# First norm of a diffusion trunk: sums of squares on VectorE, x/rms ahead of the modulation, products by feature tile, fixed orders

## The chip, the cores and the metric

The kernel runs on one core of a Trainium2 chip, in one launch. The metric is device microseconds of one execution; lower is better. Before the change three runs took 1626.13, 1631.45 and 1633.98 us, so the median is 1631.45 us.

## The reference, cut to what matters

The model is a trunk of two layers over 512 latent tokens (x) and 256 context tokens (ctx), with 1024 features, all in float32. Every sub-layer begins with an RMSNorm that is modulated by the conditioning vector:

```python
def rmsnorm(x, g):
    y = xf * lax.rsqrt(jnp.mean(xf * xf, axis=-1, keepdims=True) + NORM_EPS)
    return y * g
def modulate(h, shift, scale):
    return h * (1 + scale) + shift
...
mod_x = jnp.split(jax.nn.silu(c) @ ada_w[layer] + ada_b[layer], 6)
mod_c = jnp.split(jax.nn.silu(c_ctx) @ ada_w[layer] + ada_b[layer], 6)
h_x = modulate(rmsnorm(x, norm_g[layer, 0]), mod_x[0], mod_x[1])
h_c = modulate(rmsnorm(ctx, norm_g[layer, 0]), mod_c[0], mod_c[1])
# layer 0: projections of h_x and h_c by w_in, then differential and neighbourhood attention
```

The change touches only the start of layer 0: the modulation's shift and scale for the first norm, the norm of x and of ctx, and the first unit of projected queries, keys and values (a unit is two pairs of heads, 128 columns each of key and query, 256 of value for the first pair of units).

## The kernel before, in words

Everything lies with features on the 128 partitions, so x is 8 tiles (k = 0 to 7) of 128 features by 512 tokens and ctx is 8 tiles of 128 by 256. A product in full precision is made of three fp32r matmuls: the operand and the weight are each split into a high part and the rest, and high·high, high·rest and rest·high are added in PSUM (`wh`, `wl` are the two parts of a weight tile, `hb[k][:, 0]` and `hb[k][:, 1]` those of a feature tile).

The start of layer 0 runs like this. SyncE's queue loads x, then the modulation's weights in two halves of eight 512 KB tiles (`add_ada0(0)` and `add_ada0(1)`; each half gives shift and scale of four feature tiles, for x and ctx), with the three weight tiles of the first unit (key, query, value) between the halves and the context between those. ScalarE squares the x tiles (`sq_sum`, L324) and VectorE and GpSimd add them up; TensorE sums over partitions with a matrix of ones, and `rstd_of` (L308) makes 1/rms of it with Ln, Exp and a Newton step. `ada0_mm` (L640) multiplies the modulation tiles as they land, `ada0_h` (L647) copies the result out, transposes it, adds the bias (L249), forms the scale (L257), and calls `h_make` (L348) for each of four feature tiles: VectorE makes x times scale times 1/rms (L353), ScalarE adds the shift and rounds to the high part (L354), VectorE makes the rest (L355). `part` (L663) then multiplies those four tiles with the unit's key and query weights (512 columns wide, L667 to L669) and its value weights (256 columns, L675 to L677). Then come the sum of squares and norm of ctx, its first four tiles, the modulation's second half, the other four tiles of x, `part` again, and the last four of ctx. `keep_busy` (L212) issues products of the identity with ones whose result nobody reads.

Behind this stand, for the first unit, `qk_x` (L716: rotation by `rope_of`, L376, and splitting by `evac_pair`, L364), `qk_c` (L724: the key's, then the query's products with the context, L207 to L209, and their splitting), `v_group` (L390: the values of the context), and then the steady program of attention steps with the projections of later units between them.

Each engine runs its own queue in order. The framework that builds the program puts the instructions of each engine in an order by its own plan, from the order of the Python code and from what waits for what; `tc.issue_after(inst)` makes an instruction stand behind another in that plan. Before the change the order in this place is left to the plan. Tiles come from pools with a fixed number of buffers; a new tile waits until the readers of the tile that had its buffer are through. The one that matters here is the PSUM pool of the linear products, with two buffers:

```python
lin = st.enter_context(tc.tile_pool(name="a_lin", bufs=2, space=PSUM, reuse_waits="tile"))
linp = lambda: lin.tile([P, NX], F32, tag="lin", name="lin")
...
psk, psq = linp(), linp()
```

So the key's context products need the buffer of `psk`, which the rotation reads (L380, L381), the query's that of `psq`, and `v_group` again the buffer of the key's context products.

## Time and profile before

| what | value |
|---|---|
| median of three runs | 1631.45 us |
| the profiled execution | 1634.54 us |
| its span, first to last instruction | 1632.7 us |
| TensorE busy with matmuls | 1569.6 us, 96% of the span |
| VectorE, ScalarE, GpSimd busy | 1255.6, 747.0, 267.0 us |
| chain that ended last | TensorE 64%, VectorE 7%, DMA 4% |
| mean granted TensorE clock | 0.992 |

A profile page gives busy time per engine and shows the span in 40 equal slices (40.8 us each here), a digit for each slice in tenths of busy time. The timeline lists instructions: start and length in us, engine (PE is TensorE, DVE VectorE, ACT ScalarE, POOL GpSimd), line of the kernel, operation, output and inputs by their names in the program, shapes, and in brackets the idle time of the engine just before it and what ended that. A fp32 matmul is two records, a fp32r matmul one. The windows view gives, for stretches of the span, the busy time of each engine with the number of instructions, the granted clock (PEclk), the share of the DMA engines' time and GB/s.

### The profile page before, as it was taken

How to read it: one execution, taken by the hardware profiler on the slowest of the kernel's cores; microseconds unless marked ns; L12 is line 12 of the kernel's file. 1: busy time of each engine (PE TensorE's matmuls, PEld its weight loads, DVE VectorE, ACT ScalarE, POOL GpSimd, SP SyncE). 2: the span in 40 equal slices, each digit the busy share in tenths (PEclk: the TensorE clock that was granted, in tenths of full speed). 3: DMA queues.
4: the chain of work that ended last, by engine and by line, in shares of the span. 5: the costliest groups of instructions: out<-in, count | busy, mean ns of one | idle time of the engine just before them, and what ended most of it. 6: DMA issues, size and time to landing. Idle time of an engine off the chain costs nothing.

```text
span 1632.7 us, 26333 instructions
## 1 busy us (share of the span) xinstructions
PE 1569.6 (96%) x10222; PEld 1403.5 (86%) x10222; DVE 1255.6 (77%) x2157; ACT 747.0 (46%) x1324; POOL 267.0 (16%) x311
## 2 busy tenths in 40 slices
PE   5899998998999999999999999999999999999997
PEld 3798887886878899999999998887788899989897
DVE  4757698976688888978899867787665887869686
ACT  4446554555334532432424244456655542524344
POOL 2222222345010000010100011264322000000001
PEclk9999999999999999999999999999999999999999
DMA  9322244544235365576766753311010442323321
GB/s 343 98 57 85 89 149 129 186 139 132 72 109 154 95 183 158 152 197 168 195 180 169 211 134 95 104 53 40 14 40 27 152 132 66 125 82 104 117 78 52
DMA packets 69220, 198.48 MB, mean 122 GB/s; under 512 B 6900, under 2 KB 19348, under 8 KB 69096
## 3 DMA queue, kind: packets, MB, share of 16 engines
q1 hardware_dynamic: 59464, 164.40, 31.7%
q0 software_dynamic: 9056, 31.87, 9.1%
q8 instruction: 81, 1.33, 0.3%
q10 hardware_dynamic: 576, 0.52, 0.1%
q14 instruction: 43, 0.35, 0.1%
HBM read 160.45 MB, written 4.86 MB: 101 GB/s over the span
## 4 chain that ended last, share of the span: by engine, by line
PE 64%; DVE 7%; DMA 4%; issue 2%; ACT 2%; POOL 0%; DVEq 0%; SPq 0%; ACTq 0%; POOLq 0%
PE f L1272 5%; PE f L1274 5%; PE f L1273 5%; PE f L1685 4%; PE f L1684 4%; PE f L1683 4%; PE f L1313 3%; PE f L1314 3%; PE f L1315 3%; PE t L1517 2%; PE lin L207 2%; PE lin L208 2%; PE lin L209 2%; PE f L1737 2%; PE f L1736 2%; PE f L1738 2%
## 5 line engine op out<-in xcount | busy, mean ns | idle before, releaser
L196 ACT ACTIVATE wh<-raw 128x1024 fp32r<-128x1024 f32 (+1 forms) x96 | 92.3, 978 | 233.7 <-DVE raw L507 115.8
L207 PE MATMUL lin<-hb,wh 128*128 128x512 f32 (+1 forms) x456 | 162.8, 358 | 8.2 <-DVE q L372 2.2
L208 PE MATMUL lin<-hb,wh 128*128 128x512 f32 (+1 forms) x456 | 160.3, 352 | 0.5 <-DVE hb L197 0.4
L209 PE MATMUL lin<-hb,wl 128*128 128x512 f32 (+1 forms) x456 | 158.9, 348 | 0.0
L197 DVE TENSOR_TENSOR wl<-raw,wh 128x1024 fp32r<-128x1024 f32 (+1 forms) x96 | 106.8, 1119 | 34.9 <-ACT wh L196 32.9
L269 DVE SCALAR_TENSOR_TENSOR junk<-raw,tables 128x1024 bf16<-128x1024 f32 x80 | 97.7, 1222 | 20.2 <-DMA raw<-in_ada_wT_dram 19.9
L202 POOL DMA_DIRECT2D wl<-raw x39 | 34.1, 873 | 444.1 <-ACT wl L201 393.8
L207 PEld LDWEIGHTS lin<-hb,wh 128*128 128x128 f32 x456 | 86.4, 190 | 23.4 <-issue 4.5
L1313 PE MATMUL f<-g,wh 128*128 128x512 f32 (+1 forms) x304 | 102.8, 339 | 1.2 <-DVE q L1298 0.7
L1314 PE MATMUL f<-g,wh 128*128 128x512 f32 (+1 forms) x304 | 102.7, 339 | 0.0
L1684 PE MATMUL f<-hb,wh 128*128 128x256 f32 x360 | 101.7, 283 | 0.0
L1683 PE MATMUL f<-hb,wh 128*128 128x256 f32 x360 | 101.4, 283 | 0.0
L1685 PE MATMUL f<-hb,wl 128*128 128x256 f32 x360 | 101.2, 283 | 0.0
L1315 PE MATMUL f<-g,wl 128*128 128x256 f32 (+1 forms) x304 | 100.8, 336 | 0.0
L158 ACT CAST wh<-raw 128x1024 fp32r<-128x1024 f32 x61 | 63.9, 1047 | 77.9 <-PE lin L208 24.0
L1272 PE MATMUL f<-hb,wh 128*128 128x384 f32 x288 | 96.4, 335 | 0.9 <-ACT q L1259 0.9
L159 DVE TENSOR_TENSOR wl<-raw,wh 128x1024 fp32r<-128x1024 f32 x61 | 79.8, 1309 | 22.6 <-ACT wh L158 22.4
L208 PEld LDWEIGHTS lin<-hb,wh 128*128 128x128 f32 x456 | 86.7, 190 | 12.2 <-issue 0.9
L1274 PE MATMUL f<-hb,wl 128*128 128x384 f32 x288 | 96.3, 334 | 0.0
L1273 PE MATMUL f<-hb,wh 128*128 128x384 f32 x288 | 96.2, 334 | 0.0
L209 PEld LDWEIGHTS lin<-hb,wl 128*128 128x128 f32 x456 | 86.6, 190 | 10.4 <-issue 0.3
L339 POOL TENSOR_TENSOR ns_a<-ns_a,ns_s 128x256 f32<-128x256 f32 (+1 forms) x16 | 16.2, 1013 | 435.2 <-ACT ns_s L335 435.2
(395 smaller groups left out, 4948.7 us busy)
## 6 DMA issues: line engine op xcount, KB each, us to landing
raw<-in_w_dram SPq DMA_DIRECT2D x132, 512.0 KB, 3.7
raw<-in_ada_wT_dram SPq DMA_DIRECT2D x80, 512.0 KB, 4.2
wl<-raw POOLq DMA_DIRECT2D x39, 512.0 KB, 5.9
raw<-in_w_ab_dram SPq DMA_DIRECT2D x24, 512.0 KB, 4.2
raw<-in_ada_w_dram SPq DMA_DIRECT2D x16, 512.0 KB, 9.5
k<-k SPq DMA_DIRECT2D x16, 384.0 KB, 5.8
raw<-in_w_c_dram SPq DMA_DIRECT2D x12, 512.0 KB, 3.6
nb<-in_na_bias_dram POOLq DMA_DIRECT2D x16, 256.0 KB, 3.6
```

Source lines behind the costliest of these rows:

```text
L207: nc.tensor.matmul(ps, wh(k), xh(k), start=k == 0, stop=False)
L208: nc.tensor.matmul(ps, wh(k), xl(k), start=False, stop=False)
L209: end = nc.tensor.matmul(ps, wl(k), xh(k), start=False, stop=k == n - 1)
L1272: nc.tensor.matmul(ps, wh(k), b[:, 0, :], start=k == 0, stop=False)
L1273: nc.tensor.matmul(ps, wh(k), b[:, 1, :], start=False, stop=False)
L1274: nc.tensor.matmul(ps, wl(k), b[:, 0, :], start=False, stop=k == 3)
L1313: nc.tensor.matmul(ps, hi, g[:, 0, cols[v]], start=first, stop=False)
L1314: nc.tensor.matmul(ps, hi, g[:, 1, cols[v]], start=False, stop=False)
L1315: nc.tensor.matmul(ps, lo, g[:, 0, cols[v]], start=False, stop=last)
L1683: nc.tensor.matmul(ps, wh(k), b[:, 0, :], start=k == 0, stop=False)
L1684: nc.tensor.matmul(ps, wh(k), b[:, 1, :], start=False, stop=False)
L1685: nc.tensor.matmul(ps, wl(k), b[:, 0, :], start=False, stop=k == 3)
```

## The change

It does these things, all in the first norm and the first unit:

- The partial sums of squares of x are added by VectorE alone (`shared=False`), and the last square goes to TensorE as a third addend (`apart=True`) instead of being added first. The conditioning row is loaded and its Silu taken ahead of the squares.
- x/rms is made by itself (`scaled`), with one VectorE multiplication for each tile: four tiles ahead of the modulation's copy, four behind the first half's feature tiles. The modulation is then applied by ScalarE (`x_h`), once for the high part and once into a tile of its own, and VectorE subtracts. ctx keeps `h_make`.
- TensorE gets 44 `keep_busy` products at the start, 4 before and 14 behind the first half's transposes; the 9 behind the second half's go.
- The products run by feature tile (`part_kq(k)`, `part_v(k)`), with the second half's modulation tiles multiplied between those of k = 0 to 3.
- The loads follow one chain on SyncE's queue (`S.chain`): both halves of the modulation, then the last value weights, the context and the rotation's tables (before on GpSimd's queue, and ctx ahead of the second half). The modulation's tiles have 6 buffers of their own (before 5, and 3 of the weights' pool).
- The norm of ctx comes behind the second half: its squares stand behind tile 5's feature tile and `part_v(5)`, all eight of its tiles behind the x products; `qk_x` stands behind the last of them (`queued(h_made[-1][1])`). Scratch tiles lie in buffers of the first unit's own tiles (`Places`).

```diff
+    @contextmanager
+    def queued(*insts):
+        with ExitStack() as q:
+            for i in insts:
+                if i is not None:
+                    q.enter_context(tc.issue_after(i.ins))
+            yield
...
-            ps = ada0_mm(0)
-            rx = rstd_of(tp(), sq_sum(xr, p0), D, p0)
-            ada0_h(0, ps)
-            keep_busy(tp(), 10)
...
+            keep_busy(psk, 44)
...
+            def x_h(k, after=None):
+                t = p0.tile([P, NX], F32, tag="ns_h", name="ns_h", bufs=2)
+                with queued(after):
+                    for z in (hx[k][:, 0, :], t):
+                        act = nc.scalar.activation(z, xn[k], AF.Identity, bias=mod[0][:, 0, 0, k : k + 1], scale=amod[0][:, 0, 0, k : k + 1])
+                    return act, nc.vector.tensor_sub(hx[k][:, 1, :], t, f32(hx[k][:, 0, :]))
+
+            def scaled(ks, after=None):
+                for k in ks:
+                    with queued(after):
+                        end = nc.vector.tensor_mul(xn[k], xr[k], rx)
+                return end
...
+            ps = tp()
+            ada0_mm(ps, range(2))
+            rx = rstd_of(tp(), sq_sum(xr, px, apart=True, shared=False), D, px)
+            end, act = roots
+            four = scaled(range(4))
+            end = ada0_mm(ps, range(2, KT), end)
+            keep_busy(psk, 4, end)
+            flip, made = ada0_mod(0, ps, four)
+            keep_busy(psk, 14, flip)
...
+            last = x_h(3)
+            scaled(range(4, KT), last[1])
...
-            part(range(4))
-            rc = rstd_of(tp(), sq_sum(cr, p0), D, p1)
-            for k in range(4):
-                h_make(k, hc[k], cr[k], rc, 0, 0, 1, p0)
-            ada0_h(1, ada0_mm(1))
-            keep_busy(tp(), 9)
-            wv.append(tuple(wslice(t, 256) for t in S.next()))
-            part(range(4, KT))
-            for k in range(4, KT):
-                h_make(k, hc[k], cr[k], rc, 0, 0, 1, p0)
+            ps = tp()
+            part_kq(0)
+            ada0_mm(ps, (0,), part_v(0))
+            part_kq(1)
+            ada0_mm(ps, (1, 2), part_v(1))
+            part_kq(2)
+            ada0_mm(ps, (3, 4), part_v(2))
+            ada0_mm(ps, (5, 6, 7), part_kq(3))
+            part_v(3)
...
+            _, made = ada0_mod(1, ps)
+            ends = [x_h(k) for k in range(4, KT)]
...
+            part_kq(4)
+            part_v(4)
+            part_kq(5)
+            end = part_v(5)
+            with queued(*ends[1], end):
+                rc = rstd_of(tp(), sq_sum(cr, pc_), D, pc_)
+            part_kq(6)
+            part_kq(7)
+            ctx_h(range(KT))
+            part_v(6)
+            part_v(7)
...
-        qk_x(0, "k", psk)
-        qk_x(0, "q", psq)
+        with queued(h_made[-1][1]):
+            qk_x(0, "k", psk)
+            qk_x(0, "q", psq)
```

Behind this stretch the queues of all engines hold the same instructions in the same order as before, but for a few rows.

Three places show what moves. The first is VectorE at the end of the norm of x (`ns_v`, `ns_t`, `ns_y`, after the change `scratch`, are the steps of 1/rms; `res` is x; `ada_acc` is the copy of the modulation's first half). Before:

```order
L317 TENSOR_SCALAR ns_v_246<-t_221 128x512 [waits Activation_49]
L320 SCALAR_TENSOR_TENSOR ns_t_248<-ns_t_248,ns_v_246 128x512 [waits DVE_49,Activation_49]
L321 SCALAR_TENSOR_TENSOR ns_y_247<-ns_t_248,ns_y_247 128x512 [waits DVE_49]
L649 COPY ada_acc_255<-t_172 128x256 [waits PE_49,Pool_49]
L249 TENSOR_TENSOR mod0_116<-t_257,adab_102 128x2x2 [waits DMASW0_49,PE_49]
```

After:

```order
L351 SCALAR_TENSOR_TENSOR scratch_156<-scratch_154,scratch_156 128x512 [waits DVE_49]
L733 TENSOR_TENSOR scratch_158<-res_73,scratch_156 128x512 [waits DMAHW2_49,DVE_49]
L733 TENSOR_TENSOR scratch_158<-res_74,scratch_156 128x512 [waits DMAHW3_49]
L733 TENSOR_TENSOR scratch_158<-res_75,scratch_156 128x512 [waits DMAHW4_49]
L733 TENSOR_TENSOR scratch_159<-res_76,scratch_156 128x512 [waits DMAHW5_49]
L718 COPY ada_acc_306<-t_224 128x256 [waits PE_49]
L267 TENSOR_TENSOR mod0_117<-t_308,adab_104 128x2x2 [waits DMASW0_49,PE_49]
```

Four multiplications now stand between the last step of 1/rms and the copy.

The second is VectorE at the end of the norm of ctx (`ns_h` and `hb4` to `hb7` with 256 columns are ctx's tiles 4 to 7; `ru` and `rbuf` are the rotation's first two steps, `lin` is `psk` and then `psq`). Before:

```order
L353 SCALAR_TENSOR_TENSOR ns_h_591<-res_81,amod0_118,ns_y_410 128x256 [waits DVE_49]
L355 SCALAR_TENSOR_TENSOR hb4_128<-ns_h_587,mod0_116,hb4_128 128x256 [waits Activation_49]
L380 STREAM_SHUFFLE ru_633<-lin_304 128x512 [waits PE_49]
L355 SCALAR_TENSOR_TENSOR hb5_129<-ns_h_591,mod0_116,hb5_129 128x256 [waits Activation_49]
L381 TENSOR_TENSOR rbuf_147<-lin_304,tables_115 128x512 [waits DMASW6_49]
L353 SCALAR_TENSOR_TENSOR ns_h_595<-res_82,amod0_118,ns_y_410 128x256 [waits DMAHW0_49,DVE_49]
L353 SCALAR_TENSOR_TENSOR ns_h_599<-res_82,amod0_118,ns_y_410 128x256 [waits DVE_49]
L355 SCALAR_TENSOR_TENSOR hb6_130<-ns_h_595,mod0_116,hb6_130 128x256 [waits Activation_49]
L355 SCALAR_TENSOR_TENSOR hb7_131<-ns_h_599,mod0_116,hb7_131 128x256 [waits Activation_49]
L380 STREAM_SHUFFLE ru_642<-lin_305 128x512 [waits PE_49,Pool_49]
```

After:

```order
L385 SCALAR_TENSOR_TENSOR hb6_130<-ns_h_604,mod0_117,hb6_130 128x256 [waits Activation_49]
L385 SCALAR_TENSOR_TENSOR hb7_131<-ns_h_608,mod0_117,hb7_131 128x256 [waits Activation_49]
L410 STREAM_SHUFFLE ru_666<-lin_160 128x512 [waits PE_49]
L411 TENSOR_TENSOR rbuf_147<-lin_160,tables_71 128x512 [waits DMAHW3_49]
L410 STREAM_SHUFFLE ru_675<-lin_161 128x512 [waits PE_49,Pool_49]
L411 TENSOR_TENSOR rbuf_147<-lin_161,tables_71 128x512
L402 SCALAR_TENSOR_TENSOR k1_663<-rbuf_147,k1_663 64x512 [waits Activation_49] x2
L167 TENSOR_TENSOR wl_837<-raw_830,wh_836 128x1024 [waits DMAHW5_49,PE_49,Activation_49]
```

The key's rotation stood among ctx's tiles and now stands behind the last of them.

The third is TensorE between the unit's x products and `v_group` (`s` takes the values of x; `lin` with 256 columns takes the products with ctx). Before, the end of the query's context products and what follows:

```order
L209 MATMUL lin_685<-hb7_131,wl_297 128x256
L675 MATMUL s_306<-wh_511,hb4_128 128x256 [waits Activation_49]
L676 MATMUL s_306<-wh_511,hb4_128 128x256
L675 MATMUL s_307<-wh_511,hb4_128 128x256
L676 MATMUL s_307<-wh_511,hb4_128 128x256
L677 MATMUL s_306<-wl_512,hb4_128 128x256 [waits DVE_49]
```

After, the end of the x values and the start of the key's context products:

```order
L776 MATMUL s_162<-wl_506,hb7_131 128x256
L774 MATMUL s_163<-wh_505,hb7_131 128x256
L775 MATMUL s_163<-wh_505,hb7_131 128x256
L776 MATMUL s_163<-wl_506,hb7_131 128x256
L224 MATMUL lin_687<-hb0_124,wh_330 128x256 [waits DVE_49,Activation_49]
```

The 48 value products of tiles 4 to 7 stood behind both sets of context products and now stand ahead of them; the first context product waits for VectorE.

More of the change, by code (lines that the diff above doesn't have):

```diff
@@ L1 @@
-from contextlib import ExitStack
+from contextlib import ExitStack, contextmanager
 import concourse.bass as bass
@@ L76, in tile_trunk @@
     nc.sync.dma_start(craw, cT)
+    tables = const.tile([P, 2 * NX], F32, name="tables")
+    cost, sint = tables[:, 0:NX], tables[:, NX : 2 * NX]
+    nc.sync.dma_start(tables[0:2, :], crow)
     res_tile = lambda: xpool.tile([P, NX], F32, tag="res", name="res", bufs=KT + KT // 2 + 1)
@@ L311, in rstd_of @@
         for i, a in enumerate(accs):
-            nc.tensor.matmul(ps[:, 0:n], ones, a, start=i == 0, stop=i == len(accs) - 1)
+            end = nc.tensor.matmul(ps[:, 0:n], ones, a, start=i == 0, stop=i == len(accs) - 1)
         v = pool.tile([P, n], F32, tag="ns_v", name="ns_v")
@@ new lines, in tile_trunk @@
+            xn = []
+            for n in range(2):
+                t = place("q", 2 * NT + 128)
+                xn += [third(t, i) for i in range(3)]
+            xn += [third(k1_, i) for i in range(2)]
+            px = Places(
+                ns_a0=[third(va, 0)], ns_a1=[third(va, 1)], ns_t=[third(va, 2)],
+                ns_s=[third(vb, 0), third(vb, 1), third(k1_, 2), third(k2_, 1)], ns_v=[third(vb, 2)], ns_y=[third(k2_, 0)],
+            )
+            pc_ = Places(
+                ns_a0=[quarter(k2_, 2)], ns_a1=[quarter(k2_, 3)], ns_t=[quarter(k2_, 4)], ns_v=[quarter(k2_, 5)],
+                ns_s=[quarter(k1_, 4), quarter(k1_, 5)], ns_y=[quarter(vb, 0)],
+            )
@@ new lines, in tile_trunk @@
+            part_kq(2)
+            ada0_mm(ps, (3, 4), part_v(2))
+            ada0_mm(ps, (5, 6, 7), part_kq(3))
+            part_v(3)
+            S.request(2 * KT + 4)
+            for c in range(0, KT, 2):
+                S.start(c2[c // 2].rearrange("p (a b) -> p a b", a=2), ctxT[:, c : c + 2, :])
+            S.start(cost, rope[0, 0])
+            S.start(sint, rope[0, 1])
+            _, made = ada0_mod(1, ps)
+            ends = [x_h(k) for k in range(4, KT)]
+            pins.append((last[0], made))
```

155 lines of the change are left out of this document (98 added, 57 removed).

## The prediction

> **What bounds the kernel now.** I read the page's slices first: TensorE is full in nearly all of them, except in the first two.
>
> ```profile
> PE   5899998998999999999999999999999999999997
> ```
>
> So a shift at the start is carried to the end, and the question is when TensorE gets through the changed stretch. I take as mark the start of the second unit's key products with ctx, 86.57 us; from there both programs hold nearly the same rows. Then the windows of the start:
>
> ```profile
> 30.00:35.00 5.00, 4.13 (x12) 2.93 (x12) 5.00 (x8) 3.12 (x5) 0.03 (x1) 0.52 1.05 386
> ...
> 40.00:45.00 5.00, 5.00 (x41) 4.08 (x40) 3.29 (x8) 2.22 (x5) 0.00 (x0) 1.00 0.03 9
> ```
>
> ```profile
> 57.90:74.00 16.10, 12.88 (x98) 11.86 (x98) 14.64 (x20) 7.53 (x13) 9.90 (x10) 1.00 0.36 96
> ```
>
> From 30 to 35 us the clock (third value from the end) is at 0.52 and DMA full (1.05); at 40 us the loads are through. From 57.9 to 74 TensorE waits 3.2 us and VectorE is busy 14.64 of 16.1: there VectorE sets the pace. The timeline gives the first norm and its prices:
>
> ```profile
> 3.19 0.31 POOL masks.py:199 TENSOR_SCALAR_AFFINE_SELECT ident<-ident 128x128 f32<-128x128 f32 x1
> 12.83 1.08 PE L235 MATMUL t<-raw,craw 128*32 128x256 f32 x8 [12.83 <-DMA raw<-in_ada_w_dram]
> 15.94 3.78 PE L312 MATMUL t<-ns_a,ones 128*128 128x512 f32 x4 [0.78 <-DVE ns_a L341]
> 19.65 3.25 PE L235 MATMUL t<-raw,craw 128*32 128x256 f32 x48
> 22.53 0.69 DVE L321 SCALAR_TENSOR_TENSOR ns_y<-ns_t,ns_y 128x512 f32<-128x512 f32 x1
> 23.14 0.42 DVE L649 COPY ada_acc<-t 128x256 f32<-128x256 f32 x1
> 24.68 1.42 DVE L353 SCALAR_TENSOR_TENSOR ns_h<-res,amod,ns_y 128x512 f32<-128x512 f32 x2
> 26.53 0.50 PE L667 MATMUL lin<-hb,wh 128*128 128x512 f32 x1 [0.26 <-ACT hb L354]
> 28.82 0.50 PE L668 MATMUL lin<-hb,wh 128*128 128x512 f32 x1 [1.78 <-DVE hb L355]
> ...
> 49.52 2.17 PE L219 MATMUL t<-ones,ident 128*128 128x128 f32 x18
> 49.74 1.95 PE L219 MATMUL t<-ones,ident 128*128 128x128 f32 x16
> ```
>
> A modulation tile (8 records) takes 1.08 us at 12.83, but six in 3.25 us from 19.65: TensorE starts at half speed and is at full speed 6.8 us after its first matmul, 3.7 us after the dense stretch from 15.94. It falls back by 30 us, after waits like that of 1.78 us. Two records of an identity product more cost 2.17 - 1.95 = 0.22 us, so one is 0.22 fast and 0.44 slow. A sum product of 512 columns is 3.78 / 2 = 1.89 slow, 0.95 fast.
>
> **Part 1, up to the first product.** The 44 identity products can start when `ident` stands, at 3.5. Slow for 3.7 to 6.8 us, they do 8 to 15 in that time; the other 36 to 29 at 0.22 make 7.9 to 6.4; the end is 15.1 to 16.7, and I take 15.9. The first modulation tile has landed by 12.83, so this is a wait, but one that DMA hides: the tiles lie in six buffers, and the last is through TensorE in time. Two tiles (0.46 each, priced in part 2) bring 16.8, three sum products, fast now, 2.85: 19.6, against 19.7 before. The warm start is spent on the third addend and on waiting. 1/rms took 3.5 us from there (to 22.53 + 0.69 = 23.2), so it stands at 23.1. Now four multiplications stand ahead of the copy, 1.42 / 2 = 0.71 each, 2.8 together: the copy starts at 25.9, 2.8 later than before. From copy to modulation took 24.68 - 23.14 = 1.54: 27.4. ScalarE's high part is there at 28.2, but the transposes end at 26.8 and 14 identity products behind them hold TensorE to 29.9. By then the rest stands too (28.2 + 0.7 for the second ScalarE pass + 0.71). First product: 29.9 against 26.53, **3.4 us later**.
>
> **Part 2, tiles 0 to 3 and the second half of the modulation.**
>
> ```profile
> 45.40 3.23 PE L235 MATMUL t<-raw,craw 128*32 128x256 f32 x56
> 51.11 1.39 ACT L354 ACTIVATE hb<-ns_h,mod 128x512 fp32r<-128x512 f32 x2 [5.03 <-DVE ns_h L353]
> 51.89 0.50 PE L667 MATMUL lin<-hb,wh 128*128 128x512 f32 x1 [0.20 <-ACT hb L354]
> ...
> 73.97 0.28 PE L399 MATMUL lin<-wh,hb 128*128 128x256 f32 x1
> ...
> 79.73 0.28 PE L804 MATMUL s<-k,q 128*128 128x256 f32 x1
> ...
> 81.13 0.39 PE L207 MATMUL lin<-hb,wh 128*128 128x512 f32 x1
> ...
> 86.57 0.28 PE L207 MATMUL lin<-hb,wh 128*128 128x256 f32 x1
> ```
>
> Seven modulation tiles take 3.23, so 0.46 each. From 73.97 to 79.73 stand 48 products of 256 columns, 0.12 each; from 81.13 to 86.57 24 of 512, 0.227 each. Four feature tiles are 24 wide and 48 narrow: 5.45 + 5.76 = 11.2 us; with eight modulation tiles (3.7) and 0.5 for weight parts that come late (bounds 0 and 2): 29.9 + 15.4 = 45.3, the last modulation tile 1.4 earlier, at 43.9. Before it was 48.63 at the same work. DMA isn't the bound: before, everything had landed by 40, and now ctx and the rotation's tables (1.5 MB, 4 us at 386 GB/s) come behind. Tile 4 came out 51.89 - 48.63 = 3.3 after that; of that the copy and its hand-over (0.6) now lie beside the value products, and the VectorE pass (0.71) is gone, so 2.0 are left: the first product of tile 4 is at **47.3, 4.6 us earlier** than before. Here the densely fed TensorE keeps its clock, which is the gain that the change has.
>
> **Part 3, tiles 4 to 7.** Again 11.2 us, 0.7 for the first rest part, and the two sum products of ctx (0.48 each): 60.2. The sum products stand 11 narrow products before the end, so they are through at 58.9. Up to here the change has won: before, the 48 value products were still open here.
>
> **Part 4, the norm of ctx and what hangs on it.**
>
> ```profile
> 40.48 0.47 ACT L316 ACTIVATE ns_t<-t,epst 128x256 f32<-128x256 f32 x1 [6.95 <-PE t L312]
> 42.80 0.88 DVE L353 SCALAR_TENSOR_TENSOR ns_h<-res,amod,ns_y 128x256 f32<-128x256 f32 x2
> 45.72 0.89 DVE L355 SCALAR_TENSOR_TENSOR hb<-ns_h,mod,hb 128x256 fp32r<-128x256 f32 x2 [0.18 <-ACT hb L354]
> ...
> 57.70 0.72 DVE L380 STREAM_SHUFFLE ru<-lin 128x512 f32<-128x512 f32 x1
> 58.50 1.42 POOL L382 TENSOR_TENSOR ru<-ru,tables 128x512 f32<-128x512 f32 x1 [28.47 <-DVE ru L380]
> 58.70 0.69 DVE L381 TENSOR_TENSOR rbuf<-lin,tables 128x512 f32<-128x512 f32 x1
> 59.44 0.39 PE L207 MATMUL lin<-hb,wh 128*128 128x256 f32 x1 [1.34 <-DVE rbuf L381]
> 59.99 1.35 POOL L383 TENSOR_TENSOR rbuf<-rbuf,ru 128x512 f32<-128x512 f32 x1
> 62.08 1.27 ACT L369 ACTIVATE k<-rbuf 64x512 fp32r<-64x512 f32 x2
> 63.37 1.05 ACT L158 CAST wh<-raw 128x1024 fp32r<-128x1024 f32 x1
> 63.95 2.34 DVE L372 SCALAR_TENSOR_TENSOR k<-rbuf,k 64x512 fp32r<-64x512 f32 x2
> ...
> 68.56 0.88 DVE L372 SCALAR_TENSOR_TENSOR k<-lin,k 64x256 fp32r<-64x256 f32 x2
> 69.47 1.23 DVE L159 TENSOR_TENSOR wl<-raw,wh 128x1024 fp32r<-128x1024 f32 x1
> ...
> 71.62 1.40 DVE L372 SCALAR_TENSOR_TENSOR q<-rbuf,q 64x512 fp32r<-64x512 f32 x2
> ```
>
> Before, four ctx tiles were done by 46.6, and the context products at 59.44 waited for the rotation (`rbuf`), which frees their PSUM buffer; the value products were still there to fill. Now all of it is in a row behind 58.9, and nothing fills. Norm, as from 40.48 to 42.80: 61.3. Eight tiles, four of which took 42.80 to 46.61: 7.6, to 68.9. Rotation, 0.72 + 0.69: the key's context products start at **70.3**, 10.1 us after TensorE ran dry. They take 2.9, to 73.2. The second shuffle waits for GpSimd (69.6 + 1.42 + 1.35 and 0.1 between: 72.5), so the query's buffer is free at 73.9, and its products end at 76.8. VectorE then owes the key's rest part behind ScalarE's pass (72.5 + 1.27 = 73.8): 2.34 beside GpSimd, 1.40 without; I take 2.34, since GpSimd rotates the query then: 76.2. The weights' rest (1.23; its cast of 1.05 is done by 75) gives 77.5, the key's ctx part 78.4. That frees the buffer for `v_group`: 48 narrow, to 84.2, against 79.73 before. From there to the mark took 6.84 (the query's rest part, 1.40 behind 78.4, and the copy of k are hidden by `v_group`): 91.0 against 86.57. **Sum: 4.5 us slower.** The profiled execution of 1634.54 would become 1639.0; it lies 3.1 above the median of the three, so on the median I forecast 1631.45 + 4.5 = **1636.0 us**.
>
> The ends: with identity products ending at 15.1 (-0.8), no late weight parts (-0.5) and 1.40 for the key's rest (-0.9) it is 2.3; the other way +0.8 and +1.5 give 6.8. Sums on VectorE alone cost nothing, since 1/rms waits for TensorE. ScalarE's pass with a scale from memory isn't in the trace; L354 with a bias is 0.7 each. By the Trainium skill (ScalarE: Activation LUTs, What ACT_TABLE_LOAD costs) each such operand adds 93 ns; two passes ahead of tile 4's rest part would make the sum 4.7, and no run here shows it.
>
> **The rivals.** *Nothing waits behind part 3.* If the context products start as the x products end, the 96 narrow ones follow at 60.2, and the mark comes at 60.2 + 11.5 + 6.84 = 78.6: 8.0 us faster, 1623.5; with the early end of the identity products 8.8. The order speaks against it: the first context product has a VectorE wait, and VectorE has ctx and then the rotation. 0.08.
>
> *The clock drops* (the other side of the bound). TensorE is quiet from about 23.6 (last first-half tile near 22.7, four identity products) to 26.3, and from 60.2 to 70.3. If the first quiet drops the clock, 8 of the 14 identity products cost 0.22 more (+1.8). If the second does, the key's context products take up to 5.8, end at 76.1, and the cast (77.2), the weights' rest (78.4) and the ctx part (79.3) move `v_group` by 0.9. With +0.8 and +1.5 from above that is 9.5 us, 1641. It decides where all four come together past 8.2. For it: the clock of 0.52 at 30 to 35 came after waits under 2 us. By the Trainium skill (TensorE: Matmul & The Clock Gate, What's actually happening) the half rate returns only after an idle window of about 3.4 us; by that rule the first quiet keeps the clock, and the row above speaks against it. 0.2.
>
> *The 44 products don't raise the clock.* They end at 3.5 + 44 x 0.44 = 22.9, tiles and sums follow slowly (2.2 + 5.7, 30.8 instead of 19.6): 11.2 more, 1647. Against: the same products at 49.52 run at 0.22. 0.04.
>
> **How the numbers follow.** The forecast with its ends has 0.68. A measurement here tells 0.5% (8.2 us) from no change. Faster by that is the first rival's upper part, 0.08; slower the second and third, 0.24; the rest is 0.68. The range of 1626 to 1642 takes in the ends (1633.8 to 1638.3), most of the clock's case above and half the way to the first rival.
>
> **What would show it.** Right: first x product near 30, tile 4's near 47, TensorE idle for some 10 us before the key's first context product (released by VectorE's `rbuf`), the mark near 91. Wrong: context products that start within 3 us of the last x product, a first product before 27, a clock near 0.5 between 30 and 45.

## The result, and the profile after

The changed kernel takes 1643.62 us in the median of 11 runs (1634.99 to 1645.8), the kernel before 1629.86 in 11 runs beside it (1625.96 to 1633.98): the ratio of the means is 1.0078, 95% interval 1.0059 to 1.0096, which is 9.6 to 15.7 us slower, 12.7 in the middle. The forecast was 1636.0 with 1626 to 1642: right in the direction and, down to `v_group`, in where the time goes, too small in the size, and the measurement lies 1.6 us beyond the range. The profiled execution after took 1643.62 with a span of 1641.8.

The page's first slices, after:

```profile
PE   8689998999999999999999999999999999999997
...
PEclk9899999999999999999999999999999999999999
```

The first slice (41 us) is fuller than before (8 against 5), the second is emptier (6 against 8), and the clock is short there. The timeline of TensorE puts times to it (start, length, in brackets the wait ahead of it and who ended it):

```profile
28.83 0.48 PE L764 MATMUL lin<-hb,wh 128*128 128x512 f32 x1
...
47.44 0.73 PE L764 MATMUL lin<-hb,wh 128*128 128x512 f32 x2 [1.51 <-ACT hb L726]
...
58.18 1.02 PE L342 MATMUL t<-scratch,ones 128*128 128x256 f32 x4
...
60.23 0.28 PE L776 MATMUL s<-wl,hb 128*128 128x256 f32 x1
...
70.44 0.55 PE L224 MATMUL lin<-hb,wh 128*128 128x256 f32 x1 [9.94 <-DVE rbuf L411]
...
79.13 0.35 PE L429 MATMUL lin<-wh,hb 128*128 128x256 f32 x1 [0.55 <-DVE k L402]
...
84.95 0.40 PE L926 MATMUL s<-k,q 128*128 128x256 f32 x2
...
90.69 0.55 PE L927 MATMUL s<-k,q 128*128 128x256 f32 x1 [4.17 <-DMA k<-k]
...
98.62 0.28 PE L224 MATMUL lin<-hb,wh 128*128 128x256 f32 x1
```

The last row is the mark, the start of the second unit's key products with ctx: 98.62 against 86.57, 12.05 later, which is the whole loss of the timed runs within its interval. Down to `v_group` at 79.13 the rows are those of the forecast (28.83 for 29.9, 47.44 for 47.3, 70.44 for 70.3, 79.13 for 78.4). Behind `v_group` stands a wait that the forecast had written off: the scores with the swapped key (L927) wait 4.17 us for the copy `k<-k`. SyncE's issues show when that copy was started:

```profile
78.10 0.33 SPq L138 DMA_DIRECT2D raw<-in_w_ab_dram  x1
78.59 0.54 SPq L417 DMA_DIRECT2D k<-k  x1
79.21 0.55 SPq L418 DMA_DIRECT2D k<-k  x1
```

It is issued half a microsecond ahead of `v_group`, behind a load of 0.5 MB of weights, and TensorE is released 11.5 us after the second issue; `v_group` lasts 5.8. The windows of the quiet stretches and of what follows them (third value from the end: the granted clock):

```profile
60.30:70.40 10.10, 0.20 (x2) 0.00 (x0) 8.86 (x21) 4.90 (x11) 0.59 (x1) 0.74 0.00 0
70.40:75.30 4.90, 4.86 (x23) 4.89 (x24) 2.77 (x5) 1.26 (x2) 3.89 (x4) 0.50 0.00 0
86.50:90.70 4.20, 0.03 (x2) 0.04 (x1) 0.00 (x0) 0.00 (x0) 0.00 (x0) 0.80 0.96 223
90.70:95.90 5.20, 5.20 (x13) 4.18 (x14) 2.24 (x4) 1.99 (x4) 0.42 (x1) 0.51 0.09 36
```

After each of the two waits the products run at half clock: 4.9 us of them behind the first, 5.2 behind the second. From 84.95 to the mark it takes 13.67 us; before it was 6.84 (79.73 to 86.57). Of the 6.83 more, 4.17 are the wait, and 2.5 the half clock behind it (7.93 us from 90.69 to the mark, where 6 score products and 19 of 512 columns take 1.16 + 4.31 at full speed).

### The profile page after: what moved, and what is told of

Read it like the earlier page. It is cut to its first block, busy times and chain, and to the rows that moved or that the text cites. A ratio compares the mean times of both kernels' runs of the same rounds, so it can differ in the third digit from the quotient of the medians.

```text
span 1641.8 us, 26513 instructions
## 1 busy us (share of the span) xinstructions
PE 1578.5 (96%) x10310; PEld 1413.8 (86%) x10310; DVE 1254.8 (76%) x2158; ACT 752.4 (46%) x1332; POOL 262.8 (16%) x307
## 4 chain that ended last, share of the span: by engine, by line
PE 58%; DVE 9%; DMA 5%; issue 3%; ACT 2%; POOL 0%; DVEq 0%; ACTq 0%; POOLq 0%; SPq 0%
PE f L1809 4%; PE f L1808 4%; PE f L1807 4%; PE f L1398 4%; PE f L1396 4%; PE f L1397 4%; PE f L1438 3%; PE f L1437 3%; PE f L1439 3%; DMA wl<-raw 3%; PE t L1641 2%; PE lin L224 2%; PE lin L225 2%; PE f L1861 2%; PE f L1862 2%
## 5 line engine op out<-in xcount | busy, mean ns | idle before, releaser
L226 PEld LDWEIGHTS lin<-hb,wl 128*128 128x128 f32 x456 | 87.6, 192 | 10.4 <-issue 0.3
L166 ACT CAST wh<-raw 128x1024 fp32r<-128x1024 f32 x57 | 59.7, 1048 | 78.8 <-PE lin L225 25.8
L167 DVE TENSOR_TENSOR wl<-raw,wh 128x1024 fp32r<-128x1024 f32 x57 | 73.8, 1295 | 18.3 <-ACT wh L166 16.7
L369 POOL TENSOR_TENSOR ns_a<-ns_a,ns_s 128x256 f32<-128x256 f32 (+1 forms) x12 | 12.2, 1019 | 425.1 <-ACT ns_s L365 418.5
```

The source lines that it names most:

```text
L226: end = nc.tensor.matmul(ps, wl(k), xh(k), start=False, stop=k == n - 1)
```

## The experiments

Runs with the same start differ: the first x product after the change came between 28.58 and 30.11 in ten traces whose edits lie behind it, and tile 4 of the kernel before came at 51.89 in one trace and at 49.36 in b1, whose edit lies behind tile 4; the marks differ by as much (86.57 and 84.02). So I read stretches inside one trace. The table gives, in us of each trace, the first product of tile 4, the key's first ctx product, the first score product, the mark, and the stretch from tile 4 to the mark; the last column is the time against the kernel before on the same chip, with its interval.

| kernel | tile 4 | key ctx | scores | mark | tile 4 to mark | ratio |
|---|---|---|---|---|---|---|
| before | 51.89 | 59.44 | 79.73 | 86.57 | 34.68 | 1 |
| after | 47.44 | 70.44 | 84.95 | 98.62 | 51.18 | 1.0078 (1.0059 to 1.0096) |
| e1, swapped key by engines | 47.91 | 72.33 | 86.83 | 93.71 | 45.80 | 1.0049 (1.0031 to 1.0067) |
| e2, load behind the copy | 48.20 | 72.75 | 87.26 | 95.45 | 47.25 | 1.0040 (1.0022 to 1.0057) |
| e3, quiet stretches filled | 47.72 | 70.74 | 86.75 | 98.95 | 51.23 | 1.0069 (1.0052 to 1.0086) |
| e4, copy ahead of `scaled` | 47.38 | 71.71 | 86.23 | 99.11 | 51.73 | 1.0080 (1.0065 to 1.0095) |
| e5, value products behind key | 47.71 | 69.49 | 88.16 | 95.49 | 47.78 | 1.0073 (1.0053 to 1.0094) |
| e6, rotation free | 47.78 | 66.84 | 78.63 | 94.11 | 46.33 | 1.0065 (1.0045 to 1.0086) |
| e7, ctx early | 50.53 | 65.22 | 81.25 | 90.04 | 39.51 | 1.0046 (1.0030 to 1.0062) |
| e8, e7 + e6 + e1 | 48.99 | 62.60 | 73.14 | 88.29 | 39.30 | 1.0017 (1.0006 to 1.0029) |
| e9, e8 with shorter tail | 48.45 | 60.53 | 81.66 | 88.55 | 40.10 | 0.9998 (0.9989 to 1.0008) |
| e10, e9 with `v_group` as filler | 47.86 | 61.14 | 79.05 | 85.92 | 38.06 | 1.0008 (0.9993 to 1.0023) |
| e11, no identity products at start | 48.91 | 73.23 | 87.73 | 96.22 | 47.31 | 1.0099 (1.0070 to 1.0128) |
| b1, before with e1's edit | 49.36 | 56.91 | 77.18 | 84.02 | 34.66 | 1.0016 (1.0003 to 1.0030) |

In e6 and e8 the first score product stands ahead of `v_group`, in the others behind it. The change reaches tile 4 by 4.45 us earlier and then needs 16.5 more to the mark. The experiments take that apart.

**e1, the copy of k taken off the DMA.** In `qk_c`, for the first unit alone:

```diff
-            if key == "k":
+            if key == "k" and u == 0:
+                nc.scalar.copy(units[u]["k2"][0:64], dst[64:128])
+                nc.gpsimd.tensor_copy(units[u]["k2"][64:128], dst[0:64])
+            elif key == "k":
                 swap_halves(units[u]["k2"], dst)
```

> The mark is the start of the second unit's key products with ctx: 86.57 us before, 98.62 after the change. Theory A (the copy of k): behind v_group TensorE stands 4.17 us for the DMA copy k<-k, and the half clock that follows costs about 2.6 more; the rest of the sum was right. Here ScalarE and GpSimd make the first unit's swapped key instead of the DMA, and it stands by about 83, ahead of the scores: no wait behind v_group, the mark near 98.6 - 6.8 = 91.8, and the whole about 6.8 us (0.4%) faster than the changed kernel. Theory B (the drained TensorE's clock, wherever it waits): the same here. Theory C (the late first product, 2.3 us, is carried to the end and the copy only stands in front of another wait): the mark falls by less than 3.

TensorE's rows of e1 from the end of `v_group` on:

```profile
86.83 0.40 PE L929 MATMUL s<-k,q 128*128 128x256 f32 x2
...
90.95 0.28 PE L930 MATMUL s<-k,q 128*128 128x256 f32 x1
...
93.71 0.28 PE L224 MATMUL lin<-hb,wh 128*128 128x256 f32 x1
```

No wait and no slow product is left: 6.88 us from the scores to the mark, as before the change (6.84). From the key's ctx products to the mark it is 21.38 instead of 28.18, 6.8 less, the number that was expected. (The mark itself stands at 93.71, not at 91.8, because this run had a half-clock stretch behind tile 4 that the trace of after had not; see the last section.) The time went from 12.7 to 8.0 us above the kernel before; the two intervals just overlap.

**b1, the same edit in the kernel before.**

> The kernel before with the first unit's swapped key made by ScalarE and GpSimd instead of DMA. There the copy is issued at 69.0 and TensorE does not wait for it (the scores follow the last value product at 79.73). Theory A: hidden, so the mark stays at 86.6 within 0.3 and the time within 0.2%. If it moves by 2 us or more, the copy by engines is a gain or a loss of its own and the 6.8 us of the first experiment are not the price of the wait alone.

From the scores to the mark it takes 6.84 us with the edit (77.18 to 84.02) and 6.84 without; from the key's ctx products 27.11 against 27.13. So the copy was hidden before, and the edit is no gain of its own (1.0016, rather a small loss). With e1, the price of the wait is shown in the traces.

**e2, why the copy lands so late.** The load of weights that the trace of after issues at 78.10 is pinned behind the copy on SyncE's queue.

```diff
-                self.start(raw, src)
+                with queued(swapped[0] if len(self.raws) == 23 else None):
+                    self.start(raw, src)
...
-        nc.sync.dma_start(f32(dst[64:128]), f32(src[0:64]))
+        swapped[:] = [nc.sync.dma_start(f32(dst[64:128]), f32(src[0:64]))]
```

> The fourth load of weights (0.5 MB), which the changed kernel issues at 78.10 us just ahead of the key's swap, is queued behind it. If the copy is late because that load stands ahead of it in the transfers, it lands as in the kernel before, 8 to 9 us after its issue instead of 11 to 12: TensorE's wait of 4.17 becomes 1 to 1.5, the clock keeps, the mark is near 93 (95.5 if the clock still drops). If the copy is late only because it is issued late (78.6 against 69.0 before), nothing moves: mark 98.6.

SyncE's issues of e2 and, below, TensorE's wait for the copy and the mark:

```profile
80.90 0.54 SPq L419 DMA_DIRECT2D k<-k  x1
81.53 0.55 SPq L420 DMA_DIRECT2D k<-k  x1
82.17 6.39 SPq L138 DMA_DIRECT2D raw<-in_w_ab_dram  x3
```

```profile
88.66 0.36 PE L929 MATMUL s<-k,q 128*128 128x256 f32 x1 [1.12 <-DMA k<-k]
...
95.45 0.28 PE L226 MATMUL lin<-hb,wh 128*128 128x256 f32 x1
```

Now TensorE is released 7.1 us after the second issue instead of 11.5, waits 1.12 instead of 4.17 and keeps its clock: from the key's ctx products to the mark 22.70 instead of 28.18. In this pair of traces 3 us of the wait, and with them the clock, go with the load that stood ahead; the last 1.1 with the late issue. The size rests on one trace: in e4, e5, e6, e7 and e11, which have the load ahead of the copy as well, TensorE was released 8.6 (e11) to 11.5 us (e4) after the second issue.

**e3, the clock.** Identity products fill both quiet stretches: 40 behind the last value product (with the key's ctx products pinned behind them), 24 between the first score product and the one that waits.

```diff
+            warm = [keep_busy(tp(), 40, end)]
...
+                            kb = keep_busy(tp(), 24, mm) if (u, i, c, lo) == (0, 0, 0, 256) else None
```

> The two quiet stretches are filled with identity products whose result nobody reads: 40 behind the last value product of the x part (60.3 to about 69), 24 between the first score product and the one that waits for the swapped key (85.1 to 90.4). The waits stay. Theory A (VectorE's chain and the copy set the times): the key's ctx products take 2.9 instead of 5 us but v_group still starts at 79.1; the wait for k still ends near 90.7; the five key products that stood ahead of it now stand behind (1.2 us), and at full clock the mark is at 90.7 + 1.4 + 5.4 = 97.5. Theory B (most of the loss is the clock that drops in quiet stretches): v_group starts by 1 us or more earlier and the mark is below 96.5. If the clock falls for another reason than the quiet, the products behind 90.7 stay slow: mark near 100.

```profile
70.74 0.36 PE L224 MATMUL lin<-hb,wh 128*128 128x256 f32 x1 [1.02 <-DVE rbuf L412]
...
79.47 0.55 PE L430 MATMUL lin<-wh,hb 128*128 128x256 f32 x1 [2.17 <-DVE k L403]
```

The key's and query's ctx products are fast now, and TensorE only waits longer for VectorE's `k` ahead of `v_group` (2.17 for 0.55): from the key's first ctx product to `v_group` it takes 8.73 us, with the slow clock it took 8.69. There the half clock costs nothing, since VectorE's chain sets the time. Behind the second stretch the products are fast (92.14 to 98.95, 6.81 us, where after needs 7.93 with 5 fewer), but `v_group` began at half clock behind the longer wait, and the 24 products held TensorE to 92.1, a microsecond longer than the copy would have (an estimate: second issue at 79.56 and the 11.5 of after make 91.1). The mark is not better: of the expected 97.5 nothing came, though both halves of the reasoning show in the rows.

**e5, something to fill.** The value products of tiles 4 to 7 go behind the key's ctx products.

```diff
-            part_v(4)
...
+        end = qk_c(0, "k", [wslice(t) for t in wk])
+        with queued(end):
+            for k in range(4, KT):
+                part_v(k)
```

> The mark is the start of the second unit's key products with ctx: 86.57 us before, 98.62 after the change, 12.05 later; 6.8 of that went with the copy of k taken off the DMA. Theory D: the rest is a serial tail of VectorE behind the x part, which nothing fills. Here the 48 value products of tiles 4 to 7 stand behind the key's ctx products, as in the kernel before. TensorE is then dry from about 54 instead of 60.3; the sums of ctx come about 0.6 to 1.4 earlier, the key's ctx products start at 69 to 70; the value and query products fill to about 82, v_group to 88, by when the copy of k (issued near 77) has all but landed: mark near 95.5. Rival: the order of these products is worth nothing, since the same waits end the same chain: mark 98 to 99.

Mark 95.49, where 95.5 was expected: 3.4 us of the stretch from tile 4. The copy has all but landed by the scores (0.54 us from the first score product to the one that waits for it, where after has 5.74), though TensorE is now dry for 11.23 us ahead of the key's ctx products. The time, 1.0073, does not show the gain: its interval is all but that of the changed kernel.

**e6, the rotation free.** The pin of `qk_x` behind the last ctx tile is taken out.

```diff
-        with queued(h_made[-1][1]):
-            qk_x(0, "k", psk)
-            qk_x(0, "q", psq)
+        qk_x(0, "k", psk)
+        qk_x(0, "q", psq)
```

> The rotation of the first unit's key and query is no longer queued behind the last ctx tile; it stands ahead of the norm of ctx on VectorE, where that waits for the sums. Theory D: the PSUM buffers are free by 61, the key's ctx products follow the ctx tiles as these come (from about 64), the key's ctx part is done at about 73 instead of 79, v_group runs 73 to 79, the copy of k, issued at 73, lands near 84.5 and TensorE waits for it as before: mark 92 to 94, 5 to 6 us earlier than after the change. Rival: the rotation ahead of the norm delays the ctx tiles as much as it gains: mark 97 or later.

VectorE's rows of e6:

```profile
57.02 0.74 DVE L410 STREAM_SHUFFLE ru<-lin 128x512 f32<-128x512 f32 x1
...
61.85 2.96 DVE L402 SCALAR_TENSOR_TENSOR k<-rbuf,k 64x512 fp32r<-64x512 f32 x2
64.84 0.42 DVE L350 SCALAR_TENSOR_TENSOR scratch<-scratch 128x256 f32<-128x256 f32 x1
...
65.76 0.88 DVE L383 SCALAR_TENSOR_TENSOR ns_h<-res,amod,scratch 128x256 f32<-128x256 f32 x2
```

Mark 94.11, in the range expected, 4.9 us less from tile 4. The gain would be larger if the key's rest part (2.96) had not gone ahead of 1/rms: the first ctx tile is 4.2 us later than in VectorE's row of after:

```profile
61.56 0.88 DVE L383 SCALAR_TENSOR_TENSOR ns_h<-res,amod,scratch 128x256 f32<-128x256 f32 x2
```

**e7, ctx early.** ctx is loaded behind the first three weights, its norm made between 36 and 50 us.

```diff
+            for c in range(0, KT, 2):
+                S.start(c2[c // 2].rearrange("p (a b) -> p a b", a=2), ctxT[:, c : c + 2, :])
             wk, wq, wv = first
...
+            end = ada0_mm(ps, (3, 4), part_v(2))
+            with queued(*last, end):
+                rc = rstd_of(tp(), sq_sum(cr, pc_), D, pc_)
```

> ctx is loaded as soon as the first three weights are in, and its squares, sums and 1/rms are made in ScalarE's and VectorE's quiet from 37 to 46 us; its tiles follow the x tiles 4 to 7. The rotation stays behind the last ctx tile. Theory D: the ctx tiles are done at about 60 instead of 69, TensorE's dry stretch of 10 us shrinks to 1 or 2, v_group starts near 70 and the copy of k lands near 81.5: mark near 90. Rival: DMA is full when ctx is wanted (1.0 from 22 to 32 us), the second half of the modulation comes late and tile 4 is later by 1 us or more: mark 92 or later.

```profile
65.22 0.35 PE L224 MATMUL lin<-hb,wh 128*128 128x256 f32 x1 [2.45 <-DVE rbuf L411]
...
73.94 0.36 PE L429 MATMUL lin<-wh,hb 128*128 128x256 f32 x1 [2.16 <-DVE k L402]
...
84.47 0.36 PE L930 MATMUL s<-k,q 128*128 128x256 f32 x1 [1.66 <-DMA k<-k]
```

The dry stretch of 9.94 is 2.45, and tile 4 to the mark takes 11.7 us less than after the change, by far the most of any single edit. The rival had its part too: tile 4 came 3.1 later (the first x product 1.3 later in this run, and the sums of ctx, 1.0, ahead of the second half's end).

**e8, e9, e10, towards a better kernel.** e8 puts the edits of e7, e6 and e1 together. e9 also puts the sums behind the second half's transposes, ctx tiles between the x tiles and the key's ctx part ahead of the query's and the weights' rest parts:

```diff
+            with queued(*ends[0], flip):
+                rc = rstd_of(tp(), accs, D, pc_)
+            for k in range(5, KT):
+                ends.append(x_h(k))
+                with queued(*ends[-1]):
+                    ctx_h([k - 5] if k < 7 else range(2, KT))
...
+        k_done[:] = qk_c(0, "k", [wslice(t) for t in wk])
+        with queued(*k_done):
+            evac_pair(units[0]["q"], NC, NX, turned, -0.125)
```

e10 adds to e9, beside a pin of the query's ctx products behind the key's:

```diff
-        ps = linp().rearrange("p (t c) -> p t c", t=2)
+        ps = tp((P, 2, 256))
         v_group(ps, 0, wv)
```

> The three together: ctx early, the rotation free, the first unit's swapped key by ScalarE and GpSimd instead of DMA. If the tail and the copy are the whole loss, nothing waits for more than 2 us from 47 on: x part to 60.3, key and query with ctx to about 67, v_group to about 73, mark near 80, 6 to 7 us before the kernel before and about 0.4% faster than it. If something else stands behind (VectorE's work of 20 us between 47 and 75), the mark stays above 85.

> As the kernel with ctx early, the rotation free and the swapped key by engines (mark 88.29), with what still waited there taken away: the sums of ctx stand behind the transposes of the second half, where TensorE is idle anyway (so tile 4 is back at 47.4 from 48.99); ctx tiles go between the x tiles; the key's ctx part goes ahead of the weights' rest parts and of the query's rest on VectorE. Theory D with VectorE as the bound of this stretch: from tile 4 on VectorE has about 20 us of work, of which the key's ctx part is behind some 17; it is done near 68 instead of 73.5, v_group 68 to 74, the mark 79 to 83, 4 to 7 us before the kernel before and 0.2 to 0.4% faster than it. If the rest of the program gives the gain back, the mark is there and the time is not below the kernel before.

> The last kernel (mark 88.55, 40.1 us behind its first product of tile 4, and no faster than the kernel before) still has seven waits of 5.1 us in all between tile 4 and v_group. Here v_group gets a PSUM buffer of the small products' pool, so it no longer waits for the key's ctx part and lies between the ctx products, tile by tile; the key's ctx products all go ahead of the query's. If TensorE's waits are what is left, 3 to 5 us go: the mark 35 to 37 us behind tile 4, the time 0.15 to 0.3% below the kernel before. If VectorE's work is the bound of the stretch, v_group only fills waits that come back ahead of the scores: 39 to 40 us, the time as before.

None of the three reached its mark (80, 79 to 83, 35 to 37 behind tile 4). In e10 TensorE still stands 3.77 us for the last ctx tile, and its clock goes:

```profile
69.91 0.58 PE L227 MATMUL lin<-hb,wh 128*128 128x256 f32 x1 [3.77 <-DVE hb L387]
```

```profile
58.90:69.90 11.00, 6.67 (x47) 5.68 (x45) 10.72 (x18) 3.93 (x8) 5.51 (x4) 0.91 0.00 0
69.90:74.60 4.70, 4.70 (x22) 4.70 (x23) 2.02 (x5) 2.70 (x6) 0.73 (x1) 0.50 0.01 3
```

VectorE is busy for 10.72 of the 11.0 us ahead of it: it is the bound of this stretch once the copy and the pins are gone. Four of its eight ctx tiles were made ahead of tile 4 in the kernel before; all eight now come behind. So e9 and e10 end as fast as the kernel before (0.9998 and 1.0008), not faster. From tile 4 to the mark VectorE is busy for 27.85 us in e10 and was for 25.40 before, so I put the loss of the start's 4.5 us down to its work. That is argued from the rows; no run puts four ctx tiles back ahead of tile 4.

**e4, the start.** The copy of the modulation's first half goes ahead of the multiplications.

```diff
+                copy = nc.vector.tensor_copy(sb, ps[:, 0:256])
+                with queued(scaled([0], copy) if b == 0 else None):
+                    return ada_out(sb, tp, 4 * b)
...
-            four = scaled(range(4))
```

> The copy of the modulation's first half goes ahead of the four multiplications by 1/rms (one of them fills the transposes' shadow, the others come behind the modulation). First x product near 26.4 instead of 28.83, the following ones 1.7 to 2.4 earlier. Theory C (the start's delay is carried to the end): tile 4, the ctx norm, v_group and the mark all 1.7 to 2.4 earlier (mark 96.2 to 96.9). Rival: the second half of the modulation or the second value weights wait for DMA (0.55 us of cast wait at 43.73 was a load), then tile 4 stays at 47.4 and the mark at 98.6.

```profile
24.18 0.42 DVE L717 COPY ada_acc<-t 128x256 f32<-128x256 f32 x1 [1.46 <-PE t L252]
```

The copy now waits 1.46 for the last tile of the first half, and the first x product comes at 28.30, only 0.5 earlier; the weights' rest parts came later for it (a wait of 0.82 at 30.76), and tile 4 is where it was. So the multiplications cost less than a microsecond there, and nothing at tile 4.

**e11, no identity products at the start.**

```diff
-            keep_busy(psk, 44)
```

> The changed kernel without the 44 identity products at its start. If the first half of the modulation is bound by its loads (the last tile landed at 23.1 and waited for DMA), a cold TensorE costs next to nothing: first x product at 28.8 within 0.7, time within 0.1% of the changed kernel. Rival: the sums of squares at half speed (1.89 each instead of 0.95, three of them) put 1/rms and with it the four multiplications later: first x product 2 to 3 us later, near 31.

First x product at 30.31: between the two expectations and settled for neither, since the last modulation tile of the first half, too, came later in this run, at 23.88 behind a wait of 1.57 for its load (23.08 in the trace of after). That load was issued only at 19.51 (16.59 after): a load takes the buffer of a tile that TensorE has read, and TensorE, without the identity products, reads one tile ahead of the sums and the second behind them, at 18.81. The time, 1.0099 (1.0070 to 1.0128), does not stand apart from the changed kernel's.

## Why the prediction was right or wrong

**The bound.** Right within a few us: a shift at the start is carried to the end. The mark moved 12.05, the time by 9.6 to 15.7. From the mark to the end the fourteen traces take 1541 to 1547 us (before 1546.1, after 1543.2), so a shift of the mark by less than some 3 us, as in e9 and e10, need not show in the time.

**Part 1** (first product 3.4 later). It came 2.3 later, and the mechanism is half right. The four multiplications stand ahead of the copy and take 2.50:

```profile
22.62 2.50 DVE L733 TENSOR_TENSOR scratch<-res,scratch 128x512 f32<-128x512 f32 x4
25.04 0.42 DVE L718 COPY ada_acc<-t 128x256 f32<-128x256 f32 x1
```

The copy is at 25.04 for 25.9, 1.9 later than before, and the chain ahead was half a microsecond earlier than priced. One sentence was wrong: "the last is through TensorE in time". The last tile of the first half waits for its load and ends at 23.7 (forecast 22.7), so even without the multiplications the copy could not have started before that: in e4 it starts at 24.18, so 1.0 of the 1.9 us is the late tile's and 0.9 the multiplications'. SyncE issued the last load of this half at 12.73 before, and the last two at 15.95 and 16.59 after:

```profile
12.73 0.54 SPq L142 DMA_DIRECT2D raw<-in_ada_w_dram  x1
```

```profile
15.95 0.54 SPq L138 DMA_DIRECT2D raw<-in_ada_w_dram  x1
16.59 0.55 SPq L138 DMA_DIRECT2D raw<-in_ada_w_dram  x1
```

The half has eight tiles, and there are now six buffers where there were eight. The last two loads wait until TensorE has read the first tiles, and it reads them from 15.25 on, behind the identity products. So the wait "that DMA hides" is what held these loads back.

**Parts 2 and 3.** Tile 4 came at 47.44 (forecast 47.3), in part by luck: the first product was 1.1 early and the stretch from there took 18.6 for 17.4, 0.7 of it because the eight modulation tiles took 4.4 among the products for 3.7. Part 3 is right: the sums of ctx through at 59.2 (58.9), the last x product at 60.5 (60.2). TensorE's clock was 1.00 in this trace through the first quiet as well, which is luck: it was half for 3.4 us from 23.5 on in e10 and from 24.2 on in e11. ScalarE's pass with scale and bias from memory took 0.81 where L354 with a bias alone takes 0.72 (807 and 718 ns). The Trainium skill (ScalarE: Activation LUTs, What ACT_TABLE_LOAD costs) gives about 93 ns for each such operand: the trace agrees, with 89.

**Part 4, down to `v_group`.** Right but for 0.7 us. VectorE's rows of after:

```profile
69.00 0.72 DVE L410 STREAM_SHUFFLE ru<-lin 128x512 f32<-128x512 f32 x1
...
73.80 3.02 DVE L402 SCALAR_TENSOR_TENSOR k<-rbuf,k 64x512 fp32r<-64x512 f32 x2
76.85 1.23 DVE L167 TENSOR_TENSOR wl<-raw,wh 128x1024 fp32r<-128x1024 f32 x1
78.11 0.87 DVE L402 SCALAR_TENSOR_TENSOR k<-lin,k 64x256 fp32r<-64x256 f32 x2
```

The key's rest part took 3.02 beside GpSimd, more than the 2.34 that was taken as the upper price; the rest of the 4.5 us' sum stands row for row. Only the key's ctx products, at half clock, took 5.1 for 2.9, which cost nothing (e3). The tail comes from the order of the work, as e6 (4.9 us for the rotation) and e7 (11.7 for the late ctx) show; the two overlap and do not add.

**The step that failed** is the last: "From there to the mark took 6.84 (the query's rest part, 1.40 behind 78.4, and the copy of k are hidden by `v_group`)". It took 13.67. The copy was put at nothing without a time for its landing, and it was not hidden: 4.17 us of wait and 2.5 of half clock behind it, together nearly the whole miss of 7.6 (98.62 against 91.0; another 0.7 had come by `v_group`, with the key's rest part beside GpSimd). e1 gives these 6.8 back, and b1 shows that its edit gains nothing where the copy is in time. The numbers to see it stood in the profile of before, in the answer for the tile k:

```profile
L387 SPq DMA_DIRECT2D k<-k x1: 536/536/536, 69.0 to 69.0; - x1
L388 SPq DMA_DIRECT2D k<-k x1: 595/595/595, 69.6 to 69.6; - x1
...
DMA to landing us min/median/max: 7.8/8.4/9.0
```

Issued at 69.6, landed by 78.6, needed at 79.85: hidden by little more than 1 us. With the key's ctx part at 78.4 the copy would be issued at 78.5 to 79.1 and land near 87.5, and `v_group` ends at 84.2: 3.3 us of wait could have been in the sum. `v_group` covered it before because 4.4 us of value products stood between the issue (69.6) and `v_group` (73.97), and `v_group`'s 5.8 came on top; the change puts the value products ahead of it all. (e5 puts them back, and 0.26 us of the wait are left.) A load of weights stood ahead of the copy on the queue before, too:

```profile
68.56 0.33 SPq L142 DMA_DIRECT2D raw<-in_w_ab_dram  x1
```

So that load alone does not explain why TensorE was released 11.5 us after the second issue, where the copy of before had landed 9.0 after its issue at most. Another difference is GpSimd's load of two bias tables (0.5 MB), issued 1.9 us ahead of the copy after the change (76.71) and 7.2 ahead before (61.79); no run separates the two, and the cause of these 2.5 us stays open.

**The rivals.** *Nothing waits behind part 3* did not come: 9.94 us of wait for `rbuf`. *The 44 products don't raise the clock* did not come: the 88 records took 11.77 us and the next products were fast. *The clock drops* forecast 1641, near the result, but not by its mechanism: the first quiet kept the clock, the second lost it and that cost nothing (e3); what cost was a third drop, at the wait for the copy, which the prediction did not have.

## What to carry to other kernels

"Hidden" is a claim with two times: when the transfer lands and when it is needed. When a change moves the producer of a transfer, put the landing into the sum anew, with the row from issue to landing and with whatever the queue now has ahead of it. And work that is gathered into one row behind a stage, here eight ctx tiles, a rotation and rest parts on one engine, costs its whole length; a start that is faster by 4.5 us was worth nothing here, where it only reached that row sooner.

## What the runs showed of the hardware

A wait of the same length costs the clock in one run and not in the next. Behind tile 4's wait of 1.51 us the clock stayed at 1.00 in the trace of after; in e1 it was half for 3.4 us, and from tile 4 to the key's ctx products it takes 24.42 us for 23.00. What decides is where the wait lies on a grid. Read in steps of 0.1 us, every half-clock stretch of the fourteen traces between 20 and 110 us lasts 3.4 to 3.5, 6.9, 10.3 to 10.4 or 13.7 us: the clock changes in steps of 3.41. The windows of that grid around tile 4, in e1 and, below, in after (behind the comma: TensorE's busy time):

```profile
45.66:49.07 3.41, 1.71 (x11) 1.18 (x9) 2.14 (x7) 2.02 (x3) 0.00 (x0) 1.00 1.04 407
49.07:52.48 3.41, 3.13 (x10) 2.75 (x11) 1.05 (x3) 3.41 (x8) 0.00 (x0) 0.50 0.66 233
```

```profile
44.63:48.05 3.42, 1.91 (x15) 1.59 (x14) 1.67 (x6) 1.63 (x4) 0.00 (x0) 1.00 1.05 414
48.05:51.46 3.41, 2.94 (x19) 2.52 (x18) 1.39 (x2) 3.41 (x8) 0.00 (x0) 1.00 0.80 276
```

TensorE worked for 50% of the window in e1 and lost the clock in the next one; it worked for 56% in after and kept it. Over the whole of the fourteen traces, cut on the grid of each, the clock fell 62 times, always behind a window with 55% or less of work; it stayed full behind 6512 windows, all with 44% or more; it rose 62 times, always behind a window with 84% or more, and stayed half behind 64 with 85% or less. So in these traces it is about half a window of work that keeps the clock. In e4 the clock was still full in the wait of 4.1 us for the copy and 0.6 us beyond, and fell then, under dense work, for 3.4 us:

```profile
87.80:91.90 4.10, 0.00 (x1) 0.00 (x0) 0.00 (x0) 0.00 (x0) 0.00 (x0) 1.00 0.84 211
91.90:92.50 0.60, 0.56 (x3) 0.54 (x4) 0.00 (x0) 0.00 (x0) 0.00 (x0) 1.00 0.14 55
92.50:95.90 3.40, 3.40 (x11) 2.67 (x10) 1.96 (x3) 1.98 (x4) 0.00 (x0) 0.53 0.02 10
```

By the Trainium skill (TensorE: Matmul & The Clock Gate, What's actually happening) the clock follows a free-running window of 3413 ns, so where a wait lies in it decides; the steps of 3.41 us agree. That the half clock follows only an idle window of 3.4 us does not: the window ahead of e1's fall was half full. One such piece costs up to 1.7 us (half its length), and a kernel whose TensorE waits in several places will show it in some runs. In the eleven timed runs of the changed kernel the mean granted clock was 0.993 in the two fastest (1634.99 and 1635.54) and 0.989 in the five slowest (1643.74 to 1645.8). The 0.004 of 1640 us make 6.6, an estimate of the most that the clock adds to the spread of 11 us; what falls into waits costs nothing, and the rest of the spread was not looked at.
